# A fused attention and MLP layer on one core: the second MLP weight's block sums made in SBUF instead of DRAM

## The chip, the cores and the metric

The kernel runs on one core of one Trainium2 chip. The metric is the device time of one launch in microseconds (us), lower is better. Times before are the median of three runs; beside them one execution was taken by the hardware profiler, and all rows of the trace come from that one.

## The reference

One layer over 512 frames of width 1024, in float32. `w1` is 1024 x 4096, `w2` is 4096 x 1024.

```python
hn = rmsnorm(h, norm_mix_g[l])
proj = hn @ w_in[l]
fq, fk, fv, ff, gq, gf, gi, gg = jnp.split(proj, split_idx, axis=-1)
...
fox_out = fox_attention(to_heads(fq), to_heads(fk), to_heads(fv), log_f)   # 8 heads of 64, causal, log-forget bias
rec = hgrn2_chunkwise(gq, gf, gi, lbs[l])                                  # gated linear recurrence, 4 heads
...
h = h + jnp.concatenate([fox_out, rec], axis=-1) @ w_out[l]
h = h + memory_cross_attention(rmsnorm(h, norm_x_g[l]), mem_n, w_xq[l], w_xkv[l], w_xo[l])
u = rmsnorm(h, norm_ff_g[l]) @ w1[l]
h = h + jnp.square(jax.nn.relu(u)) @ w2[l]
return rmsnorm(h, final_norm_g)
```

## The kernel before

Every matrix product runs in three passes on TensorE (PE): operands are split into a high part and a low part of a 32-bit format that PE multiplies faster (`float32r`), and high x high, high x low and low x high are added up in PSUM. So every weight that comes from DRAM is loaded raw by a DMA on SP's queue, its high part is made by ScalarE (ACT, line 178) and its low part by VectorE (DVE, line 182). Four buffers hold the high parts (`wh`) and four the low parts (`wl`); a split can start when the product four units earlier has left its buffers.

The stages follow one another on PE, whose order is written out by hand: the projections by `w_in` with the recurrence, the forgetting attention (softmax in 16 steps of two heads, with projections and the memory's keys and values run between as filler), `w_out`, the cross attention, and the MLP. The order on the other engines is made by a scheduler at build time.

The MLP's hidden width of 4096 is cut into eight groups of 512. For groups 2 to 7 the product with `w1` ("u"), and for all groups the product with `w2` ("d"), are computed by a scheme with seven block products instead of eight (`PRODUCTS`, in the order 1, 5, 6, 2, 7, 3, 4). Three of the seven take a plain quarter of the weight block, 00, 10 or 11 (`QUAD`); the other four take sums of quarters: "5" is 00+01, "7" is 01+11, "6" is 5+11, "4" is 6+10 (`SUMS`). On PE the order is: the "u" products of group g+1, then the "d" products of group g. Groups 6 and 7 of "d" are interleaved at the end.

The sums of weights do not depend on the input, and before the change all are made by DMAs from DRAM to DRAM, issued by GpSimd (POOL): `sum_jobs` gives eight DMAs for each group and weight, a copy (line 427) and an accumulation (line 425) for each of the four sums, 512 KB each. `Presum` paces them: `tick` counts PE's matmul time, and `PACE` says from which count on one goes out how often.

```python
RAWS, HB, LOADS = 5, 4, 7
PACE = (25.0, 4.0), (106.0, None), (183.0, 3.0), (306.0, 6.0)
```

In the attention loop, where the pace is off, each of the 16 steps issues one instead. Each sum DMA waits for the PE instruction at which it was counted. POOL also makes the softmax's bias rows (`fox_bias`), small powers, sums of squares, and the output's first scaling (`fa`, line 1599).

In the MLP, `unit` hands out split weights: it prepares four units ahead and loads seven ahead (`LOADS`), raw blocks going to five buffers in turn, two of the pool `wr` and three of the shared pool `s4` (twelve buffers of 512 KB, which also hold the accumulators, hidden parts `hb` and much else). `hidden_sums` combines the squared hidden values on DVE for the seven products, `add_to` adds a product's PSUM bank to the accumulators; banks U, V and Y take several products each (`PLAN`), and a copy of U to V is made by ACT after product "1".

Small pools: `q2` holds four tiles of 256 KB (the queries' parts, later the final gain `gfin`), `t3` two.

Of the kernel before, what the change touches and what calls it, by code (L numbers as in the profile page):

```python
# [9 lines left out]
F32 = mybir.dt.float32  # L10
R = mybir.dt.float32r
# [26 lines left out]
X1, X2, X3, X4 = 1.5, 2.0, 1.5, 2.0  # L38
NEG = -3.0e38
SEVEN = (2, 3, 4, 5, 6, 7)  # L40
RAWS, HB, LOADS = 5, 4, 7
PACE = (25.0, 4.0), (106.0, None), (183.0, 3.0), (306.0, 6.0)


@with_exitstack
def emit(
# [32 lines left out]
    ap_ = ctx.enter_context(tc.tile_pool(name="ap", bufs=4))  # L79
    s4p = ctx.enter_context(tc.tile_pool(name="s4p", bufs=12))  # L80
    k4p = ctx.enter_context(tc.tile_pool(name="k4p", bufs=4))
    q2p = ctx.enter_context(tc.tile_pool(name="q2p", bufs=4))
    t3p = ctx.enter_context(tc.tile_pool(name="t3p", bufs=2))
    t2p = ctx.enter_context(tc.tile_pool(name="t2p", bufs=10))
    s3p = ctx.enter_context(tc.tile_pool(name="s3p", bufs=3))
    smp = ctx.enter_context(tc.tile_pool(name="smp", bufs=16))
# [12 lines left out]
    def k4(shape, name, dt=F32):  # L99
        return k4p.tile([P] + shape, dt, tag="k4", name=name)  # L100

    def q2(name):
        return q2p.tile([P, S], R, tag="q2", name=name)

    def t3(name):
        return t3p.tile([P, S], F32, tag="t3", name=name)

    def t2(name, dt=F32, shape=(S,)):
        return t2p.tile([P] + list(shape), dt, tag="t2", name=name)
# [344 lines left out]
            return us  # L454

    presum = Presum()
    for g in range(DFF // HG):
        presum.jobs.append(sum_jobs("d", g))
        if g + 2 in SEVEN:
            presum.jobs.append(sum_jobs("u", g + 2))  # L460
    park = {}

    ms0 = sm(NT, "ms0")
# [344 lines left out]
    def fox_proj(p):  # L808
        wt = next_panel()

        fq[p] = [q2(f"q{p}{j}") for j in range(2)]
        ps = mm(f"pq{p}")
        yield from gemm_fm(ps, wt, 0, hn_hi, hn_lo)
        t = t3(f"qs{p}")
# [11 lines left out]
        t = t3(f"ks{p}")  # L826
# [25 lines left out]
    def fox_rows(p):  # L852
        for h in (2 * p, 2 * p + 1):
            fF[h] = t2(f"nF{h}")
            ac.dma_start(fF[h], Fd[h, :].partition_broadcast(P))

    mt = []

# [198 lines left out]
    for n in range(len(pairs) + 2):  # L1057
        if n < len(pairs):
            p, tb = pairs[n]
            if tb == 0:  # L1060
                fill.until(f"proj{p}")
                if p == 0:
                    fill.add(proj_tm(new_fv(), WT, AF.Identity, "fv"), "fv256")
                    fill.add(fox_proj(2), "proj2")
                elif p == 1:
                    fill.add(mem_v(0))
                    fill.add(fox_proj(3), "proj3")
                elif p == 2:
                    fill.add(mem_v(1))
                    for i in range(4):  # L1070
                        fill.add(mem_k(i))
        if n >= 3 and n % 2 == 1:
            for step in pairs[n - 3 : n - 1]:
                fox_out(*step)
        if 1 <= n <= len(pairs):
            for j in range(2):
                fox_T((*pairs[n - 1], j))
        if n == 0:
            me_hi.extend(s4([4, M], f"meh{t}", R) for t in range(2))
            me_lo.extend(s4([4, M], f"mel{t}", R) for t in range(2))  # L1080
        elif n <= KC // 2:
            mem_T(2 * n - 2)
        if n < len(pairs):
            fox_scores(*pairs[n])
            if n + 1 < len(pairs):
                fox_biases(n + 1)
            dma = presum.emit()
            if dma is not None:
                tc.keep_in_program_order(dma)
            if tb == 2 and p < 3:  # L1090
                fox_rows(p + 1)
        fill.run(FX[min(n // NT, 1)][n % NT])
# [75 lines left out]
    def x_proj(h):  # L1168
        wt = next_panel()
        xq[h] = []  # L1170
        for i in range(2):
            ps = mm(f"xq{h}{i}")
            yield from gemm_fm(ps, wt, i * P, x1_hi, x1_lo)
            a, b = q2(f"xqh{h}{i}"), q2(f"xql{h}{i}")
# [101 lines left out]

    gfin = [q2p.tile([P, S], F32, tag="q2", name=f"gfin{i}") for i in range(2)]
    for i in range(2):  # L1280
        gp.dma_start(gfin[i], final_norm_g[i * S : (i + 1) * S].partition_broadcast(P))
    HS = S // 2
    units, unit_q = {}, deque()
    sqs, comb, hbs = {}, {}, {}
# [3 lines left out]

    def raw_tile(name):
        raw_n[0] += 1  # L1290
        if raw_n[0] % RAWS in (0, 2):
            return wrp.tile([P, D], F32, tag="wr", name=f"wr{name}", padded_shape=[P, UK * UW])
        return s4([D], f"wr{name}")

    load_q = deque()

    def add_unit(key, shape, src):

        name = "".join(map(str, key))
        box = []  # L1300

        def load():
            raw = raw_tile(name).rearrange("p (k n) -> p k n", k=shape[0])
            nc.sync.dma_start(raw, src())
            box.append(raw)

        def prep():
# [313 lines left out]
    def mlp_up_group(g):  # L1621
# [3 lines left out]
        for j in range(2):  # L1625
# [72 lines left out]
```

## Time and profile before

| | |
|---|---|
| median of 3 timed runs | 766.57 us (764.31 to 767.61) |
| the profiled execution, its own time | 761.13 us |
| its span, first to last instruction | 759.4 us |
| PE busy | 747.1 us (98%) |
| DVE, ACT, POOL busy | 533.4, 429.9, 227.0 us |
| mean granted TensorE clock | 0.999 |
| DMA moved | 162.86 MB, 64.52 of it by POOL's queue |

How to read the rows: a group row has line, engine, operation, output <- input, and after the x the number of instructions; a DMA row has the size of one and the median time from issue to landing; a row of a stretch has its bounds, its length, then for PE, PEld (the weight load), DVE, ACT and POOL the busy time and the number of instructions, then the granted clock, the DMA engines' busy share and GB/s. In the chain and the timeline a row starts with its start and its duration. A row of the waits gives the total, the number and the longest. Tile names have their numbers cut: `wrd` is a raw block of `w2`, `wru` of `w1`, `whd` and `wld` its high and low part, `wsd` and `wsu` sums in DRAM, `hb` a hidden part, `nF` a bias row, `mt` the memory, `bi` and `pt` the softmax and its transpose.

### The profile page before, as it was taken

What the parts mean: (1) busy time and instruction counts of PE and PEld (TensorE: products, weight loads), DVE (VectorE), ACT (ScalarE), POOL (GpSimd) and SP (SyncE); (2) the same over time, 40 slices, a digit from 0 to 9 for tenths busy, and PEclk for the clock granted to TensorE, in tenths of its full rate; (3) what the DMA queues carried; (4) which work ended last, traced back from release to release, by engine and by line L of the source; (5) the groups of instructions that cost most, each with busy time, mean ns of one, the idle gap of its engine ahead of it and who ended that gap; (6) DMA issues with size and microseconds to landing.
All of it is one profiled execution on the core that took longest, in us unless ns stands there. A gap on an engine that the chain in (4) does not pass through costs nothing.

```text
span 759.4 us, 12056 instructions
## 1 busy us (share of the span) xinstructions
PE 747.1 (98%) x4501; PEld 649.1 (85%) x4501; DVE 533.4 (70%) x844; ACT 429.9 (57%) x715; POOL 227.0 (30%) x322
## 2 busy tenths in 40 slices
PE   9999999999998999999999999999999999999996
PEld 6889888898887988888888888898989999998985
DVE  5647873676876755545555558888788787979697
ACT  5655564565664643335443476657575757574873
POOL 7218552353453426841112211111111110000014
PEclk9999999999999999999999999999999999999999
DMA  8676877676788799996679969898988998948342
GB/s 249 195 222 132 209 191 167 183 159 159 194 255 216 232 221 265 236 253 152 151 212 182 242 159 306 178 356 220 289 263 290 226 291 267 274 146 276 113 139 111
DMA packets 99580, 162.86 MB, mean 214 GB/s; under 512 B 6481, under 2 KB 67450, under 8 KB 99074
## 3 DMA queue, kind: packets, MB, share of 16 engines
q0 software_dynamic: 27968, 64.52, 38.9%
q1 hardware_dynamic: 69810, 94.43, 37.4%
q10 hardware_dynamic: 1744, 3.15, 1.3%
q8 instruction: 35, 0.57, 0.3%
q14 instruction: 23, 0.19, 0.1%
HBM read 157.87 MB, written 62.93 MB: 291 GB/s over the span
## 4 chain that ended last, share of the span: by engine, by line
PE 95%; DMA 2%; DVE 1%; ACT 1%; issue 1%; POOL 0%; ACTq 0%; SPq 0%
PE U L1504 4%; PE U L1503 4%; PE U L1505 4%; PE uU L1378 3%; PE uU L1377 3%; PE uU L1376 3%; PE xq L243 2%; PE wo L243 2%; PE xq L244 2%; PE xq L245 2%; PE xw L245 2%; PE xw L244 2%; PE xw L243 2%; PE u L245 2%; PE wo L244 2%; PE u L244 2%
## 5 line engine op out<-in xcount | busy, mean ns | idle before, releaser
L182 DVE TENSOR_TENSOR wld<-wrd,whd 128x1024 fp32r<-128x1024 f32 x56 | 68.5, 1225 | 19.4 <-ACT whd L178 19.4
L178 ACT ACTIVATE whd<-wrd 128x1024 fp32r<-128x1024 f32 x56 | 59.2, 1057 | 26.1 <-PE uV L1377 8.0
L425 POOL DMA_DIRECT2D wsd<-in_w_dram x32 | 34.7, 1084 | 104.0 <-PE uU L1378 22.1
L178 ACT ACTIVATE whu<-wru 128x1024 fp32r<-128x1024 f32 x42 | 44.4, 1057 | 36.5 <-PE uU L1377 16.6
L182 DVE TENSOR_TENSOR wlu<-wru,whu 128x1024 fp32r<-128x1024 f32 x42 | 50.5, 1228 | 12.8 <-ACT whu L178 12.8
L1503 PE MATMUL U<-whd,hb 128*128 128x512 f32 x120 | 46.8, 390 | 0.0
L1504 PE MATMUL U<-wld,hb 128*128 128x512 f32 x120 | 46.8, 390 | 0.0
L1505 PE MATMUL U<-whd,hb 128*128 128x512 f32 x120 | 46.7, 389 | 0.0
L425 POOL DMA_DIRECT2D wsu<-in_w_dram x24 | 28.5, 1186 | 53.9 <-PE xq L245 8.7
L987 POOL TENSOR_SCALAR bi<-nF,Ft 128x128 f32<-128x128 f32 (+3 forms) x32 | 22.5, 707 | 47.2 <-PE pt L1019 26.0
L1599 POOL TENSOR_TENSOR fa<-acc,gfin 128x512 f32<-128x512 f32 x4 | 6.5, 1654 | 86.2 <-DVE acc L1469 83.9
L427 POOL DMA_DIRECT2D wsd<-in_w_dram x16 | 10.9, 680 | 56.8 <-PE gq L245 14.5
L1378 PE MATMUL uU<-x_hi,wlu 128*128 128x256 f32 x96 | 27.2, 283 | 0.0
L1377 PE MATMUL uY<-xs_lo,whu 128*128 128x256 f32 x96 | 27.2, 283 | 0.0
L1378 PE MATMUL uU<-xs_hi,wlu 128*128 128x256 f32 x96 | 27.2, 283 | 0.0
L1376 PE MATMUL uY<-xs_hi,whu 128*128 128x256 f32 x96 | 27.2, 283 | 0.0
L1378 PE MATMUL uY<-xs_hi,wlu 128*128 128x256 f32 x96 | 27.2, 283 | 0.0
L1376 PE MATMUL uU<-xs_hi,whu 128*128 128x256 f32 x96 | 27.2, 283 | 0.0
L1377 PE MATMUL uU<-xs_lo,whu 128*128 128x256 f32 x96 | 27.2, 283 | 0.0
L1377 PE MATMUL uU<-x_lo,whu 128*128 128x256 f32 x96 | 27.2, 283 | 0.0
L1376 PE MATMUL uU<-x_hi,whu 128*128 128x256 f32 x96 | 27.1, 283 | 0.0
L1133 ACT ACTIVATE x_hi<-hT,gv 128x512 fp32r<-128x512 f32 x16 | 11.4, 715 | 27.5 <-DVE hT L1132 27.4
(996 smaller groups left out, 2679.4 us busy)
## 6 DMA issues: line engine op xcount, KB each, us to landing
wsd<-in_w_dram POOLq DMA_DIRECT2D x48, 512.0 KB, 6.5
wsu<-in_w_dram POOLq DMA_DIRECT2D x36, 512.0 KB, 6.7
wrd<-wsd SPq DMA_DIRECT2D x32, 512.0 KB, 5.2
wrd<-in_w_dram SPq DMA_DIRECT2D x24, 512.0 KB, 6.1
wru<-wsu SPq DMA_DIRECT2D x24, 512.0 KB, 4.8
wru<-in_w_dram SPq DMA_DIRECT2D x18, 512.0 KB, 5.9
wsd<-wsd POOLq DMA_DIRECT2D x16, 512.0 KB, 5.5
wsu<-wsu POOLq DMA_DIRECT2D x12, 512.0 KB, 5.1
```

What stands on the lines that cost most here:

```text
L178: ac.activation(hi, raw, AF.Copy)
L182: ve.tensor_tensor(lo, raw, f(hi), ALU.subtract)
L243: te.matmul(ps, wh, hi, start=n_ == 0 and not begun, stop=False)
L244: te.matmul(ps, wh, lo, start=False, stop=False)
L245: at = te.matmul(ps, wl, hi, start=False, stop=k == order[-1])
L425: yield gp.dma_start(dst, block(g, b), accum_op=ALU.add)
L1376: te.matmul(ps[:, i, :], whi[:, k, ws], xh[:, k, :], start=begin, stop=False, skip_group_check=True)
L1377: te.matmul(ps[:, i, :], whi[:, k, ws], xl[:, k, :], start=False, stop=False, skip_group_check=True)
L1378: at = te.matmul(ps[:, i, :], wlo[:, k, ws], xh[:, k, :], start=False, stop=k == UK - 1, skip_group_check=True)
L1503: te.matmul(ps, hi, whi[:, k, :], start=begin, stop=False, skip_group_check=True)
L1504: te.matmul(ps, hi, wlo[:, k, :], start=False, stop=False, skip_group_check=True)
L1505: at = te.matmul(ps, lo, whi[:, k, :], start=False, stop=k == 1, skip_group_check=True)
```

## The change

W2 sums of groups 0 to 6 are no longer made in DRAM. `chain_begin(g)` loads five blocks of `w2` into SBUF (`a1` and `c1` = 00, `a2` = 01, `b2` = 11, `b1` = 10) and accumulates `a2 += 11` and `c1 += 01` from DRAM by POOL's DMAs. The split of product "1" reads `a1`; then `a1 += a2` makes the sum for "6" in place. The split of "2" reads `b1`; then `b1 += a1` makes the sum for "4". "5" reads `c1`, "7" reads `a2`, "3" reads `b2`. A chain begins when the first "u" unit of group g+1 is prepared, and group 0's before the MLP starts.

W1 sums of groups 2 to 7 and the W2 sums of group 7 stay in DRAM. `PACE` starts them at a count of 183, past the attention, every 3 us, and from 306 on every 10 us; the attention loop issues none. At most three raw loads (`RAWS`) wait for their split, in two buffers of `wr` and one of `s4`.

The pools `q2` and `t3` become `q4` (two tiles of 512 KB) and `t4` (one), which also hold `b1` and `b2`. The bias rows `nF` are loaded by POOL's queue and no longer by ACT's, the final gain by one DMA.

```diff
-RAWS, HB, LOADS = 5, 4, 7
-PACE = (25.0, 4.0), (106.0, None), (183.0, 3.0), (306.0, 6.0)
+RAWS, HB = 3, 4
+PACE = (183.0, 3.0), (306.0, 10.0)
...
-    q2p = ctx.enter_context(tc.tile_pool(name="q2p", bufs=4))
-    t3p = ctx.enter_context(tc.tile_pool(name="t3p", bufs=2))
+    q4p = ctx.enter_context(tc.tile_pool(name="q4p", bufs=2))
+    t4p = ctx.enter_context(tc.tile_pool(name="t4p", bufs=1))
...
-    for g in range(DFF // HG):
-        presum.jobs.append(sum_jobs("d", g))
-        if g + 2 in SEVEN:
-            presum.jobs.append(sum_jobs("u", g + 2))
+    for g in SEVEN:
+        presum.jobs.append(sum_jobs("u", g))
+    presum.jobs.append(sum_jobs("d", NG - 1))
...
-            ac.dma_start(fF[h], Fd[h, :].partition_broadcast(P))
+            gp.dma_start(fF[h], Fd[h, :].partition_broadcast(P))
...
-            dma = presum.emit()
-            if dma is not None:
-                tc.keep_in_program_order(dma)
...
-        if raw_n[0] % RAWS in (0, 2):
+        if raw_n[0] % RAWS:
             return wrp.tile([P, D], F32, tag="wr", name=f"wr{name}", padded_shape=[P, UK * UW])
         return s4([D], f"wr{name}")
...
         def prep():
             while not box:
                 load_q.popleft()()
+            if key[0] == "u" and key[1] not in chain:
+                chain_begin(key[1] - 1)
+            waiting[0] -= 1
...
+    chain = {}
+    RAW = {"1": "a1", "2": "b1", "5": "c1", "3": "b2", "6": "a1", "7": "a2", "4": "b1"}
+
+    def chain_begin(g):
+
+        chain[g + 1] = w = {}
+        for name, rc in (("a1", "00"), ("c1", "00"), ("a2", "01"), ("b2", "11"), ("b1", "10")):
+            if name == "b2":
+                t = t4(f"wb2{g}")
+            elif name == "b1":
+                t = q4(f"wb1{g}", F32)
+            else:
+                t = s4([2, S], f"w{name}{g}")
+            w[name] = t
+            nc.sync.dma_start(t, block2(g, rc))
+        gp.dma_start(w["a2"], block2(g, "11"), accum_op=ALU.add)
+        gp.dma_start(w["c1"], block2(g, "01"), accum_op=ALU.add)
+
+    def add_chain(g, name):
+
+        def prep():
+            w = chain[g + 1]
+            unit = new_parts([2, S], f"d{g}{name}")
+            with ahead(PW):
+                split_of(unit[0], unit[1], w[RAW[name]])()
+            if name == "1":
+                gp.dma_start(w["a1"], w["a2"], accum_op=ALU.add)
+            elif name == "2":
+                gp.dma_start(w["b1"], w["a1"], accum_op=ALU.add)
+            units["d", g, name] = unit
+
+        unit_q.append((("d", g, name), prep))
...
     def down_units(gs):
         for name in PRODUCTS:
             for g in gs:
+                if g < NG - 1:
+                    add_chain(g, name)
+                    continue
                 add_unit(("d", g, name), [2, S], lambda g=g, name=name: block2(g, QUAD[name]) if name in QUAD else wsum["d", g, name])
...
-        while load_q and len(order) - len(load_q) < at + LOADS:
+        while load_q and waiting[0] < RAWS:
             load_q.popleft()()
...
+    chain_begin(0)
     ups = mlp_up_group(0)
```

More of the change, by code (lines that the diff above doesn't have):

```diff
@@ L100, in k4, with q4, t4 @@
         return k4p.tile([P] + shape, dt, tag="k4", name=name)
[L102 to L106, printed above, removed]
+    def q4(name, dt=R):
+        return q4p.tile([P, 2, S], dt, tag="q4", name=name)
+    def t4(name):
+        return t4p.tile([P, 2, S], F32, tag="t4", name=name)
     def t2(name, dt=F32, shape=(S,)):
@@ L809, in fox_proj @@
         wt = next_panel()
-        fq[p] = [q2(f"q{p}{j}") for j in range(2)]
+        q, ts = q4(f"q{p}"), t4(f"qk{p}")
+        fq[p] = [q[:, j, :] for j in range(2)]
         ps = mm(f"pq{p}")
         yield from gemm_fm(ps, wt, 0, hn_hi, hn_lo)
-        t = t3(f"qs{p}")
+        t = ts[:, 0, :]
         ve.scalar_tensor_tensor(t, ps, 0.125, rbc, op0=ALU.mult, op1=ALU.mult)
@@ L825, in fox_proj @@
         yield from gemm_fm(ps, wt, P, hn_hi, hn_lo)
-        t = t3(f"ks{p}")
+        t = ts[:, 1, :]
         ve.tensor_tensor(t, ps, rbc, ALU.mult)
@@ L1173, in x_proj @@
             yield from gemm_fm(ps, wt, i * P, x1_hi, x1_lo)
-            a, b = q2(f"xqh{h}{i}"), q2(f"xql{h}{i}")
+            ab = q4(f"xq{h}{i}")
+            a, b = ab[:, 0, :], ab[:, 1, :]
             ac.activation(a, ps, AF.Copy)
@@ L1269, in emit @@
     run_now(rest())
-    gfin = [q2p.tile([P, S], F32, tag="q2", name=f"gfin{i}") for i in range(2)]
-    for i in range(2):
-        gp.dma_start(gfin[i], final_norm_g[i * S : (i + 1) * S].partition_broadcast(P))
+    gfin = q4("gfin", F32)
+    gp.dma_start(gfin.rearrange("p h n -> p (h n)"), final_norm_g.partition_broadcast(P))
+    gfin = [gfin[:, i, :] for i in range(2)]
     HS = S // 2
@@ L1290, in raw_tile @@
         raw_n[0] += 1
-        if raw_n[0] % RAWS in (0, 2):
+        if raw_n[0] % RAWS:
             return wrp.tile([P, D], F32, tag="wr", name=f"wr{name}", padded_shape=[P, UK * UW])
         return s4([D], f"wr{name}")
-    load_q = deque()
+    load_q, waiting = deque(), [0]
     def add_unit(key, shape, src):
@@ L1305, in load @@
             box.append(raw)
+            waiting[0] += 1
         def prep():
```

## The prediction

> **What bounds the kernel now.** I read the page first, then who TensorE (PE) waited for, the table of stretches, the chain that ended last, the DMA issues, and last the rows of one MLP group.
>
> ```profile
> span 759.4 us, 12056 instructions
> PE 747.1 (98%) x4501; PEld 649.1 (85%) x4501; DVE 533.4 (70%) x844; ACT 429.9 (57%) x715; POOL 227.0 (30%) x322
> ```
>
> PE works 747.1 of 759.4 us. The change touches no matmul: in the built program PE's instructions stand in the same order as before. So it can only win back PE's idle time, 12.3 us, or add to it. Where that idle time lies, first by what ended it, then by stretch (in each row the second number is the stretch, the third PE's busy time):
>
> ```profile
> PE pt L1019 <- DVE dn L1010: 3.1, 1, 3.1
> PE pst L906 <- DVE rec L927: 1.5, 1, 1.5
> PE warm L355 <- DVE ones L359: 1.3, 1, 1.3
> ...
> 125.00:150.00 25.00, 23.37 (x146) 20.35 (x145) 13.98 (x32) 13.10 (x41) 8.43 (x14) 1.00 0.54 170
> 225.00:250.00 25.00, 21.95 (x155) 19.20 (x155) 17.36 (x40) 14.10 (x28) 9.08 (x16) 1.00 0.80 214
> 575.00:600.00 25.00, 25.00 (x191) 24.16 (x190) 17.72 (x21) 17.18 (x24) 3.15 (x3) 1.00 0.99 286
> 750.00:760.00 10.00, 3.16 (x26) 2.91 (x24) 4.96 (x12) 2.78 (x5) 1.82 (x4) 0.88 0.56 210
> ```
>
> PE has two holes in mid-kernel, 1.63 us (25 - 23.37) and 3.05 us (25 - 21.95), both before the MLP. The rest is the first and the last microseconds, which the change leaves as they are. In the MLP, of which 575 to 600 is a sample, PE has no hole at all: the list above names no other wait. The granted clock is 1.00 in all these stretches but the last. The chain shows what made the two holes (start, duration):
>
> ```profile
> 118.07 0.63 POOL wsu L425
> 118.70 8.46 DMA mt<-in_mem_dram
> 134.64 1.13 PE pst L906 x8
> 231.12 8.23 DMA wr19a<-in_w_xkv_dram
> 239.37 1.07 ACT wh19a L178
> 243.50 1.22 PE pt L1019 x8
> ```
>
> Both are late transfers. The load of `mt` is queued on POOL behind a block sum (L425), travels 8.46 us, and holds up ScalarE (ACT) on the way to `pst`. The load of `wr19a` travels 8.23 us; ACT stands at its split, and the softmax behind it on ACT comes late for `pt`.
>
> **Part by part: sums taken out of the way of the attention.**
>
> ```profile
> wsd<-in_w_dram POOLq DMA_DIRECT2D x48, 512.0 KB, 6.5
> wsu<-in_w_dram POOLq DMA_DIRECT2D x36, 512.0 KB, 6.7
> wrd<-wsd SPq DMA_DIRECT2D x32, 512.0 KB, 5.2
> wrd<-in_w_dram SPq DMA_DIRECT2D x24, 512.0 KB, 6.1
> ...
> wsd<-wsd POOLq DMA_DIRECT2D x16, 512.0 KB, 5.5
> wsu<-wsu POOLq DMA_DIRECT2D x12, 512.0 KB, 5.1
> nF<-Fd ACTq DMA_DIRECT2D x8, 256.0 KB, 4.7
> ```
>
> Before: 48+36+16+12 = 112 sum DMAs. After: 8 for each of the six W1 groups and 8 for W2 group 7, 56, and the first of them stands on POOL behind the last softmax bias. So all sums that run beside the projections and the attention go, and the two late loads have the engines of the DMA more to themselves. Neither hole should survive a load that comes some 3 us sooner: 1.63 + 3.05 = 4.7 us gained. What is late next: in the first place nothing, since ACT was waiting for `mt` alone; in the second the bias rows `nF`, which move from the ACT queue to POOL. They land in 4.7 us by the row, and their issue on POOL costs time in which POOL makes no bias; but POOL is busy 9.08 of 25 us there, so I cost that at nothing (if this cover is gone, some 1 us of the 3.05 stays). One new W2 load (`wb20`) also goes ahead of `wr19a` in SP's queue; its transfer takes the place of sums that are gone. The smaller gain, one hole closed and not the other, is 1.6 us; below nothing there is no mechanism here that the rows show.
>
> From 183 us of counted matmul time on, sums go out every 3 us, the same pace as before, only W1's; PE had no hole in that stretch, and I cost it at nothing. Joining pools (`q2`, `t3`) keeps the bytes and the users in pairs: nothing.
>
> **Part by part: W2 sums made in SBUF.** Per group g of 0 to 6, 8 sum DMAs in DRAM and 7 loads become 5 loads on SP and 4 accumulating DMAs on POOL: 15 transfers become 9, so the MLP's DMA queues get lighter. What is new is a chain within the group. The accumulation `a1 += a2` may start only when the split of product "1" has read `a1`, and the split of "6" must wait for it; `b1 += a1` sits likewise between the splits of "2" and "4". ACT and VectorE (DVE) take their work in order, so a late "6" split delays all that is queued behind it. How long may such a DMA take? Rows of a typical group (its product "1" starts on PE at 597.08):
>
> ```profile
> 589.61 1.23 DVE L182 TENSOR_TENSOR wld<-wrd,whd 128x1024 fp32r<-128x1024 f32 x1 [1.65 <-ACT whd L178]
> 594.29 1.05 ACT L178 ACTIVATE whd<-wrd 128x1024 fp32r<-128x1024 f32 x1
> 599.16 0.62 ACT L1346 ACTIVATE sq<-sq 128x512 f32<-128x512 f32 x1
> 599.81 0.69 DVE L1437 TENSOR_TENSOR s<-sq,sq 128x512 f32<-128x512 f32 x1 [0.34 <-ACT sq L1346]
> 604.81 1.35 DVE L1471 SCALAR_TENSOR_TENSOR acc<-U,acc 128x512 f32<-128x512 f32 x2
> 607.99 0.39 PE L1503 MATMUL U<-whd,hb 128*128 128x512 f32 x1
> 609.60 1.23 DVE L182 TENSOR_TENSOR wld<-wrd,whd 128x1024 fp32r<-128x1024 f32 x1
> 613.42 0.39 PE L1503 MATMUL U<-whd,hb 128*128 128x512 f32 x1
> ```
>
> The split of "1" has read its block at 589.61 + 1.23 = 590.84. The split of "6" starts at 594.29 today; call its start S. From it to the end of the square at 599.16 + 0.62 lie 5.49 us of ACT work, and DVE then works through the hidden sums (from 599.81) to the first subtraction from bank U, which ends half-way through the pair at 604.81, at 605.49: 5.68 us. PE's product "7" writes bank U at 607.99 and must find it read: S + 5.49 + 0.03 + 5.68 <= 607.99, S <= 596.8. The same DVE run on to the low half for "4" (609.60 + 1.23) is 11.02 us, needed 0.23 us after 613.42: S <= 597.1. So from POOL's issue to landing there are 596.8 - 590.84 = 5.9 us free; every us more is a us of PE per group. Of the seven chains five (groups 1 to 5) have this shape; group 0's splits come a whole long panel ahead, and group 6's products are interleaved with group 7's and twice as far apart.
>
> No row shows an accumulation in SBUF. The nearest are these: accumulations in DRAM (L425, whole run, then MLP alone), copies on the same queue (L427), and stores out of SBUF on it (L491); minimum, median and maximum time to landing.
>
> ```profile
> L425 POOL DMA_DIRECT2D wsd<-in_w_dram x32: 1026/1074/1229, 59.9 to 652.2; - x32
> DMA to landing us min/median/max: 6.1/7.6/11.2
> ```
>
> ```profile
> L425 POOL DMA_DIRECT2D wsd<-in_w_dram x11: 1026/1058/1080, 488.1 to 652.2; - x11
> DMA to landing us min/median/max: 6.1/8.1/11.2
> ```
>
> ```profile
> L427 POOL DMA_DIRECT2D wsd<-in_w_dram x16: 607/686/735, 41.0 to 573.3; - x16
> DMA to landing us min/median/max: 3.8/5.2/7.8
> ```
>
> ```profile
> L491 POOL DMA_DIRECT2D xTd<-xT x4: 531/550/804, 14.2 to 29.3; - x4
> DMA to landing us min/median/max: 2.9/3.3/4.5
> ```
>
> The bounds are 2.9 us (the fastest plain transfer of this size out of SBUF) and 11.2 us. My value: a transfer out of SBUF, 3.3, plus what accumulating adds to a copy, 7.6 - 5.2 = 2.4: an estimate of 5.7 us. I stay near it and not near 8.1, because at the time of `a1 += a2` the W2 loads of the group are long done and half the sums are gone. 5.7 lies just inside 5.9; single landings scatter by about 1 us (2.9 to 4.5), so I charge 0.1 us for each of the five groups, 0.5 us. At 2.9 us it costs nothing (a gain is excluded, PE has no hole there); at 8.1 it costs 5 x 2.2 = 11.0 us.
>
> The Trainium skill (DMA: Bandwidth & Descriptors, section "Anatomy of one DMA — SWDGE (gpsimd) path") gives every DMA issued by GpSimd about 2.0 us plus its bytes over 436 GB/s. By it 512 KB would take an estimated 3.2 us and the chain would cost nothing at all, so the sum would be 4.7 us of gain. The L491 row agrees with it, the L425 rows (7.6 us for the same bytes) do not, and what an accumulation within SBUF takes no row here shows; I keep the estimate from the rows.
>
> What waits behind a waiting instruction: on POOL, the next group's two accumulations from DRAM and the remaining W1 and group 7 sums, needed tens of us later; on SP, the next group's loads of `a1` wait until `b1 += a1` has landed, and behind them stand W1 loads. Only three raw buffers are left for these, where there were five; but the W2 loads that shared them are gone, and I cost it at nothing. If each group lost a us there, it would be 5 us, which the range holds.
>
> **Sum.** -4.7 + 0.5 = -4.2 us. The profiled execution took 761.13 us (span 759.4); -4.2 makes it 756.9. The median of the timed runs is 766.57, 5.4 above the profiled one, and the profile does not show why; I take the same 4.2 off it: **762.4 us**, 0.55% faster.
>
> **The rivals.** About 0.5% (3.8 us) is what a measurement of this kernel can tell from no change.
> *A: sums in SBUF land no sooner than sums in DRAM.* For it: the accumulation itself adds 2.4 us whatever the place, and the MLP rows have a median of 8.1. Against it: source and target are both on the core, and the queues are lighter. Price: 5 x (8.1 - 5.9) = 11.0; 766.57 - 4.7 + 11.0 = 772.9 us. It turns slower than before at a landing of 5.9 + 4.7/5 = 6.8 us, and by more than 0.5% at 5.9 + 8.5/5 = 7.6 us.
> *B: gain and loss cancel.* One hole stays, because the bias rows now come through POOL's queue or the panel loads are slow by themselves (the plain loads `wrd<-in_w_dram` also take 6.1 us), so that only 1.6 us are won: 765.0 us; or both close and the accumulations take 6 to 7.6 us. Against it: the two loads that made the holes took 8.46 and 8.23 us, well above 6.1.
>
> **How the numbers follow.** The forecast gets 0.45, B 0.23, A 0.32; the same three numbers are the chances of faster by over 0.5%, within it, and slower by over it, since the forecast and A lie beyond it. Low end: the timed runs were 5.4 us above the profiled one, and if most of that is the same two waits grown longer it goes too: 766.57 - 4.7 - 4 = 758. High end: A with a landing of 8.9 us, some of the slower rows: 5 x 3.0 = 15.0, 766.57 - 4.7 + 15.0 = 777. The forecast's own range is 758 to 764.
>
> **What would show it.** Right: PE's list of waits loses `pst` and `pt`, `mt` lands in well under 8 us, PE is busy 25.00 of 25 us in every MLP stretch, and the accumulations `wa<-wa` and `wb<-wa` land in under 5.9 us. Wrong: holes of PE in the MLP at "6", "7" or "4", ended by DVE or ACT, with ACT's `whd` waiting for `wa<-wa`; or the holes near 133 and 241 us still there.

## The result and the profile after

The change makes the kernel slower: 807.89 us (804.51 to 808.48) against 764.67 us (763.36 to 767.61) for the kernel before in the same session, ratio 1.0546, 95% interval 1.0515 to 1.0576. The forecast was 762.4 us, 0.5% faster. The profiled execution took 807.47 us, its span is 46.4 us longer than before. Three executions of the runs below (2643.37, 1245.18 and 791.02 us) were disturbed, and medians and ratios leave them out.

The head of the page, PE's list of waits, and six stretches of the kernel after:

```profile
span 805.8 us, 11988 instructions
PE 761.4 (95%) x4501; PEld 659.2 (82%) x4501; DVE 534.2 (66%) x844; ACT 428.2 (53%) x715; POOL 215.6 (27%) x301
```

```profile
PE uU L1414 <- ACT uV L1420: 28.3, 5, 8.5
PE uU L1414 <- ACT uY L1425: 3.8, 2, 2.5
...
PE U L1541 <- DVE acc L1509: 1.2, 2, 0.6
...
PE pt L1019 <- DVE bi L1011: 0.7, 1, 0.7
```

```profile
125.00:150.00 25.00, 25.00 (x160) 22.31 (x159) 15.71 (x34) 14.87 (x49) 7.40 (x13) 1.00 0.31 93
150.00:175.00 25.00, 24.31 (x169) 22.38 (x168) 16.91 (x45) 15.15 (x38) 9.71 (x22) 1.00 0.20 61
225.00:250.00 25.00, 24.95 (x188) 22.19 (x188) 20.01 (x49) 15.84 (x33) 9.32 (x18) 1.00 0.58 181
500.00:525.00 25.00, 19.42 (x141) 19.02 (x140) 9.94 (x10) 11.03 (x15) 1.65 (x2) 0.86 0.85 221
550.00:575.00 25.00, 16.50 (x127) 16.30 (x126) 10.82 (x11) 11.33 (x16) 2.49 (x3) 0.86 0.87 219
600.00:625.00 25.00, 21.18 (x142) 20.45 (x141) 10.32 (x11) 12.58 (x17) 1.96 (x2) 0.86 0.76 217
```

The attention did what was forecast. Both holes are gone, the one of `pst` and the one of `pt` near 241 us (24.95 of 25 us), and `mt`, which travelled 8.46 us, now lands in 3.6. The 0.7 us that the list still has at `pt` is a new hole near 164 us, in a stretch (150 to 175) where PE had none before. PE's instructions stand in the same order in both kernels, so the same matmul can be compared: the one that started at 246 us before starts 4.1 us sooner.

From there to the MLP's sevenfold products 2.0 us of this are lost again, in small waits. These products, from 496 us on, then lose 47.7 us (from 2.1 us ahead to 45.6 behind). The MLP now has a hole in every group of "u", always ahead of a product that reuses bank U: in five groups "6" (in the first of them "7" as well, 1.2 us), in one "7". PE waits there for ACT's copy of U to V (or Y). And the granted clock, 1.00 before, is 0.86 in these stretches. The copy itself takes 0.58 us; what ACT does ahead of it is seen in its rows at the longest hole (the product "1" of this group starts at 545.67), with SP's rows below:

```profile
543.26 1.05 ACT L178 ACTIVATE whu<-wru 128x1024 fp32r<-128x1024 f32 x1
545.87 0.63 ACT L1490 ACTIVATE hb<-n 128x512 fp32r<-128x512 f32 x1 [1.57 <-PE U L1543]
557.55 2.00 ACT L178 ACTIVATE whu<-wru 128x1024 fp32r<-128x1024 f32 x2 [11.04 <-DMA wru<-in_w_dram]
559.46 0.58 ACT L1420 ACTIVATE uV<-uU 128x512 f32<-128x512 f32 x1
```

```profile
536.34 0.38 SPq L1334 DMA_DIRECT2D wa<-in_w_dram  x1
536.82 0.48 SPq L1334 DMA_DIRECT2D wc<-in_w_dram  x1
537.40 0.41 SPq L1334 DMA_DIRECT2D wa<-in_w_dram  x1
539.18 0.37 SPq L1334 DMA_DIRECT2D wb<-in_w_dram  x1
540.00 0.34 SPq L1302 DMA_DIRECT2D wru<-wsu  x1
542.11 0.37 SPq L1334 DMA_DIRECT2D wb<-in_w_dram  x1
545.04 6.27 SPq L1302 DMA_DIRECT2D wru<-in_w_dram  x3
```

ACT's queue has the splits of "2" and "7" ahead of the copy. The split of "2" stands idle for 11.04 us until its raw W1 block lands. SP issued that load at 545.04, when "1" of the same group was about to start on PE, because only then a raw buffer came free, and after the five loads of the next chain (L1334) had gone out; it landed at 557.5. So "6", whose own weights were ready, waits for a copy that waits for a block that "6" does not use.

The time to landing (minimum, median, maximum) of W1 raw blocks, first before, then after. The profile shows it for 11 of the 42 blocks in each, and for no more than that in the runs below:

```profile
DMA to landing us min/median/max: 3.2/5.3/8.2
```

```profile
DMA to landing us min/median/max: 3.3/7.4/12.4
```

It is not that more is moved: the whole kernel moves 140.84 MB, where it was 162.86. From 480 to 705 us, before and after:

```profile
480.00:705.00 225.00, 225.00 (x1430) 205.30 (x1429) 185.75 (x228) 145.08 (x193) 23.21 (x27) 1.00 0.85 255
```

```profile
480.00:705.00 225.00, 193.75 (x1145) 174.31 (x1144) 151.43 (x187) 114.85 (x155) 29.14 (x29) 0.93 0.76 204
```

The DMA engines are less busy on average (0.76 against 0.85), but the transfers come in bursts: in the six microseconds in which the late block of the group above is issued they are full (share 1.03, first row). Full engines alone are not the trouble, though. The kernel before has stretches as full (second row) without a hole, with five raw buffers:

```profile
545.00:551.00 6.00, 6.00 (x49) 5.88 (x48) 5.88 (x9) 0.63 (x1) 2.27 (x2) 1.00 1.03 261
546.00:552.00 6.00, 6.00 (x53) 6.00 (x52) 2.45 (x2) 3.72 (x5) 1.19 (x1) 1.00 1.08 334
```

The accumulations within SBUF, which the prediction worried about, mostly landed in time (`a1 += a2`, then `b1 += a1`):

```profile
L1346 POOL DMA_DIRECT2D wa<-wa x7: 877/917/1036, 469.3 to 754.1; - x7
DMA to landing us min/median/max: 4.5/4.8/7.5
```

```profile
L1348 POOL DMA_DIRECT2D wb<-wa x7: 852/865/882, 480.0 to 772.2; - x7
DMA to landing us min/median/max: 4.5/4.5/6.1
```

Two of the seven `a1 += a2` took longer than the 5.9 us allowed (7.45 and 7.00). In these two groups ACT's split of "6" waits for them, and PE then stands 0.6 us ahead of a "d" product for DVE's `acc`, as the prediction had said; that is the 1.2 us in the list above.

### The profile page after: what moved, and what is told of

It reads as the page before. It is cut to its first block, busy times and chain, and to the rows that moved or that the text cites. A ratio compares the mean times of both kernels' runs of the same rounds, so it can differ in the third digit from the quotient of the medians.

```text
span 805.8 us, 11988 instructions
## 1 busy us (share of the span) xinstructions
PE 761.4 (95%) x4501; PEld 659.2 (82%) x4501; DVE 534.2 (66%) x844; ACT 428.2 (53%) x715; POOL 215.6 (27%) x301
## 2 busy tenths in 40 slices
DMA packets 94572, 140.84 MB, mean 175 GB/s; under 512 B 5793, under 2 KB 66762, under 8 KB 94290
## 5 line engine op out<-in xcount | busy, mean ns | idle before, releaser
L1414 PE MATMUL uU<-xs_hi,whu 128*128 128x256 f32 x96 | 32.9, 343 | 32.1 <-ACT uV L1420 28.3
L1414 PEld LDWEIGHTS uU<-xs_hi,whu 128*128 128x128 f32 x96 | 23.1, 241 | 33.5 <-ACT uV L1420 29.3
L182 DVE TENSOR_TENSOR wld<-wa,whd 128x1024 fp32r<-128x1024 f32 x21 | 25.7, 1222 | 16.2 <-ACT whd L178 16.1
L178 ACT ACTIVATE whd<-wa 128x1024 fp32r<-128x1024 f32 x21 | 22.1, 1051 | 18.4 <-DMA wa<-wa 8.9
L1415 PE MATMUL uU<-xs_lo,whu 128*128 128x256 f32 x96 | 31.7, 330 | 0.0
L1416 PE MATMUL uU<-xs_hi,wlu 128*128 128x256 f32 x96 | 31.5, 328 | 0.0
L1346 POOL DMA_DIRECT2D wa<-wa x7 | 6.4, 920 | 88.7 <-DVE wld L182 88.7
L182 DVE TENSOR_TENSOR wld<-wb,whd 128x1024 fp32r<-128x1024 f32 x21 | 26.8, 1274 | 4.5 <-ACT whd L178 4.5
L1541 PEld LDWEIGHTS U<-whd,hb 128*128 128x128 f32 x120 | 22.5, 188 | 8.5 <-issue 2.1
```

The source lines that it names most:

```text
L178: ac.activation(hi, raw, AF.Copy)
L182: ve.tensor_tensor(lo, raw, f(hi), ALU.subtract)
L1346: gp.dma_start(w["a1"], w["a2"], accum_op=ALU.add)
L1414: te.matmul(ps[:, i, :], whi[:, k, ws], xh[:, k, :], start=begin, stop=False, skip_group_check=True)
L1415: te.matmul(ps[:, i, :], whi[:, k, ws], xl[:, k, :], start=False, stop=False, skip_group_check=True)
L1416: at = te.matmul(ps[:, i, :], wlo[:, k, ws], xh[:, k, :], start=False, stop=k == UK - 1, skip_group_check=True)
```

## The experiments

Theories for the 47.7 us lost in the MLP: T1, three raw buffers are too few; T2, W1 loads stand behind the chain's loads in SP's queue; T3, the chain's seven transfers come as a burst and fill the DMA engines just when W1 blocks are needed. The W2 sums' landing in SBUF is rival A of the prediction. The ratios are to the kernel before, measured beside each run.

**All sums late, but in DRAM.**

```diff
-PACE = (25.0, 4.0), (106.0, None), (183.0, 3.0), (306.0, 6.0)
+PACE = (183.0, 2.0), (306.0, 5.0)
...
-            dma = presum.emit()
-            if dma is not None:
-                tc.keep_in_program_order(dma)
```

> The kernel before with all its DRAM sums (W1 and W2, 112 transfers) issued past the attention (from 183 us of counted matmul time, one every 2 us, from 306 us one every 5 us) and nothing else of the change: no sums in SBUF, five raw buffers. If the gain came from taking sums out of the attention alone, the holes of 1.63 us (pst) and 3.05 us (pt) go and the MLP keeps its five raw buffers: 760 us, 4 to 5 us below before. Rival: the gain needs the lighter DMA queues of the SBUF sums; then the denser sums between 183 and 306 us make holes of their own, and the time is 765 us or more.

776.92 us, ratio 1.0164 (1.0128 to 1.0200). The rival holds for this pace: both attention holes are gone or small (225 to 250 us is 25.00 of 25), but from 300 to 350 us PE is busy for 41.76 of 50, because POOL's sum of squares comes late among the sums issued every 2 us:

```profile
PE pm L1149 <- POOL ssq L1139: 7.0, 1, 7.0
PE pt L1019 <- DVE bi L1011: 0.7, 1, 0.7
```

The second row is the new hole of the changed kernel: PE is busy 24.31 of 25 us from 150 to 175 here too. The bias rows still come by ACT's queue in this run, so their move to POOL's is not what made it.

Sums taken out of the attention have to go somewhere; here the new place cost more than the old one.

**Five raw buffers** (two more in the pool `wr`; the room comes from `t2` and `sm`).

```diff
-RAWS, HB = 3, 4
+RAWS, HB = 5, 4
-    wrp = ctx.enter_context(tc.tile_pool(name="wrp", bufs=2))
+    wrp = ctx.enter_context(tc.tile_pool(name="wrp", bufs=4))
...
```

> The changed kernel with five raw buffers instead of three (the room is taken from two small pools, so the attention may lose some us). Theory T1, too few raw buffers: a W1 block is loaded when the buffer of the block three products earlier is split, 8.6 us ahead of its use, and lands in 7 to 12 us; with five buffers the load starts 5.8 us sooner, the five holes before product 6 (28.3 us) and the slow matmuls behind them (14 us) go: 760 to 768 us. Theory T3, the DMA engines are full at the start of each group (five loads and two accumulations of the chain beside the W1 loads): the loads are late all the same, and over half of the 46 us stay: above 785 us.

787.56 us, ratio 1.0314 (1.0277 to 1.0350). Between the two. The wait for the copy to V is gone, a part has moved on to the copy to Y, behind the next late split:

```profile
PE uU L1414 <- ACT uY L1425: 13.2, 4, 6.4
PE pv L1035 <- ACT pts L1023: 7.1, 7, 2.0
```

The second row is the price of the smaller pools in the attention (PE 92.15 of 100 us from 175 to 275). Compared matmul by matmul, the MLP alone loses 19.0 us here instead of 47.7. Two buffers more give back 29 us, though W1 blocks take no less time to land (median 9.8 us); they are issued sooner.

**Chain loads on POOL's queue.**

```diff
-            nc.sync.dma_start(t, block2(g, rc))
+            gp.dma_start(t, block2(g, rc))
```

> The changed kernel with the five loads of each chain issued from GpSimd's queue instead of SP's, so that no W1 load stands behind them; three raw buffers as in the change. Theory T2, the W1 loads of products 7 and 2 are late because they stand in SP's queue behind the chain's five loads: the holes go, 760 to 770 us. Theory T1 (a buffer comes free too late) and T3 (DMA engines full): the load of product 2 still waits for its buffer and still takes about 12 us; holes before product 6 stay, 795 to 815 us.

808.47 us, ratio 1.0585 (1.0542 to 1.0629): nothing gained. Compared matmul by matmul the MLP loses 44.0 us instead of 47.7; these 3.7 us are lost again ahead of it, where from 400 to 475 us PE is busy for 71.96 of 75. So T2 is at most a small part: it matters that the transfers are under way at this time, and much less in whose queue they stood.

**ACT's copy ahead of the splits.** The splits of "2" and "7" are prepared one product later and kept behind the copy in ACT's order.

```diff
-        while unit_q and len(order) - len(unit_q) < at + 4:
+        while unit_q and len(order) - len(unit_q) < at + (3 if key[0] == "u" and key[2] == "1" else 4):
...
+                if what == "hl pin":
+                    tc.keep_in_program_order(ins)
```

> The changed kernel with ScalarE's copy of bank U (product 1) put ahead of the splits of products 2 and 7 in ScalarE's queue. If the late raw load reaches PE only through this copy, PE goes on with product 6 (2.9 us) and then stands before product 2 for what is left: each of the five holes becomes 2.9 us shorter and moves from product 6 to product 2 or 7, and product 6 no longer runs at half clock; 785 to 797 us. If the holes had another cause than the late split (the copy itself, or PSUM), they go altogether: below 770 us.

796.71 us, ratio 1.0439 (1.0397 to 1.0481). As expected, at the upper end: the waits are still 25.1 us (32.1 in the change), but now stand further on.

```profile
PE uU L1416 <- ACT uY L1427: 15.6, 5, 5.3
PE uV L1416 <- ACT whu L178: 6.8, 4, 3.7
PE uV L1418 <- DVE wlu L184: 2.7, 4, 0.8
```

The last two rows are "2" waiting for its own split. So the copy only handed the lateness on; that cost 9 us of the 47.7 (the MLP loses 38.7 here, matmul by matmul).

**No chain loads from group 1 on** (constants instead).

```diff
-            nc.sync.dma_start(t, block2(g, rc))
+            if g > 0:
+                gp.memset(t, 0.01)
+            else:
+                nc.sync.dma_start(t, block2(g, rc))
+        if g > 0:
+            return
```

> The changed kernel with the five loads and the two accumulations from DRAM of groups 1 to 6 left out: GpSimd fills the five tiles with a constant instead (so W2 of these groups is not the real one), and the accumulations within SBUF stay. Three raw buffers as in the change, 42 transfers fewer. Theory T1, three raw buffers are too few in themselves (a block is loaded 8.6 us ahead of its use, less some 2.3 us for the two splits, and lands in 7 us or more even without the chain): holes of 1 us or more stay in the MLP, 775 to 800 us. Theory T3, the loads are late only because the chain's seven transfers fill the DMA engines at the start of each group: W1 blocks land in under 6 us, the holes go, 757 to 766 us.

769.16 us, ratio 1.0046 (1.0017 to 1.0074). W1 blocks land in 4.3 us (median), and the longest hole is 1.7 us, still with three buffers:

```profile
PE uU L1419 <- ACT uY L1430: 2.2, 2, 1.1
PE uU L1419 <- ACT uV L1425: 1.7, 1, 1.7
...
DMA to landing us min/median/max: 3.2/4.3/5.6
```

Compared matmul by matmul the MLP loses 8.8 us (from 3.6 ahead to 5.2 behind) instead of 47.7: 39 us of the loss need the chain's transfers. That is what T3 says, but the run takes away the bytes together with the burst (118.81 MB are moved in all, not 140.84), so it cannot tell these two apart. The rest, small holes, is what three buffers leave even without them, somewhat more than T3 alone had forecast.

**No accumulations within SBUF** (both left out).

```diff
-            if name == "1":
-                gp.dma_start(w["a1"], w["a2"], accum_op=ALU.add)
-            elif name == "2":
-                gp.dma_start(w["b1"], w["a1"], accum_op=ALU.add)
```

> The changed kernel with the two accumulations within SBUF of each chain left out (so products 6, 7 and 4 of W2 use blocks without the last addend); all loads stay. This prices rival A of the prediction. By the trace they landed in 4.8 and 4.5 us, within the 5.9 us that the chain allows: 802 to 809 us, nothing gained beyond scatter. If the accumulations were the cost, or held up SP's queue through the buffers that they keep: 795 us or less.

794.02 us, ratio 1.0354 (1.0321 to 1.0386): 14 us gained, where I had expected none. The waits are of the same kind, only shorter, and still ahead of "6" of "u":

```profile
PE uU L1410 <- ACT uV L1416: 22.9, 5, 6.8
```

So the accumulations cost something, though not by landing late ahead of a "d" product. My theory for it was SP's queue, which waits for `b1 += a1` before it can load the next `a1`. A spare block buffer and each accumulation alone were to show it.

**A spare block buffer** (room again from `t2` and `sm`).

```diff
-    s4p = ctx.enter_context(tc.tile_pool(name="s4p", bufs=12))
+    s4p = ctx.enter_context(tc.tile_pool(name="s4p", bufs=13))
```

> The changed kernel with one block buffer more (13 instead of 12; the room is taken from two small pools), so that the first load of the next group's chain need not wait until the accumulation into b1 has read a1. Leaving out the accumulations within SBUF gained 14 us. If that was because SP's queue stands at this wait and issues the burst of chain loads some 3 to 6 us later, into the first W1 loads of the next group: 790 to 798 us here, with the sums still made. If the accumulations cost by their own traffic, or by W2 blocks that come late: 803 us or more.

803.14 us, ratio 1.0514 (1.0469 to 1.0559). This does not tell the two apart: the first load no longer waited for it, but the next tile, `c1`, got the buffer that `a1` had left, and SP stood there from 535.8 to 540.7 us.

**Only `b1 += a1` left out, and only `a1 += a2` left out.**

```diff
-            elif name == "2":
-                gp.dma_start(w["b1"], w["a1"], accum_op=ALU.add)
```

```diff
-            if name == "1":
-                gp.dma_start(w["a1"], w["a2"], accum_op=ALU.add)
-            elif name == "2":
+            if name == "2":
```

> The changed kernel with only the accumulation of a1 into b1 left out (so product 4 of W2 uses a block without the other addends); the one of a2 into a1 stays. In SP's queue the next chain's first load, into a1's buffer, then no longer waits until this accumulation has landed. If the 14 us that both accumulations cost are this wait, which pushes the chain's loads into the next group's first W1 loads: 790 to 799 us. If the cost is another: 803 us or more.

> The changed kernel with only the accumulation of a2 into a1 left out (so products 6 and 4 of W2 use blocks without an addend); the one of a1 into b1 stays, and SP's queue still waits for it. If the wait in SP's queue is the cost, nothing is gained: 802 to 809 us. If the accumulations cost by their landing ahead of product 6: 798 us or less.

803.71 us (ratio 1.0506, 1.0486 to 1.0526) and 799.30 us (1.0438, 1.0392 to 1.0483). Both against my theory: the first gained 4 us where 9 to 18 were forecast, the second 8 to 9 where none was. In the first, SP's wait moved to the second load of the chain once more (same group as above; "1" of "u" starts about 1 us earlier):

```profile
530.91 0.38 SPq L1334 DMA_DIRECT2D wa<-in_w_dram  x1
535.53 0.38 SPq L1334 DMA_DIRECT2D wc<-in_w_dram  x1
536.00 0.42 SPq L1334 DMA_DIRECT2D wa<-in_w_dram  x1
```

With both left out, `c1`'s load goes at 532.13, 11.0 us ahead of "1" of the next group; in the change it goes at 536.82, 8.9 us ahead of it. The load of "2" then goes 2.8 us ahead of "1" instead of 0.6, and takes no less time to land (12.8 us, 12.4 in the change). That fits SP's queue as a part of the cause, but it is one group, and how the 14 us divide into that wait and the accumulations' own traffic stays open.

**Four raw buffers and both copies first; then the chain's transfers spread as well.** The first has `RAWS` 4 (room again from `t2` and `sm`) and the copies after "1" and "6" ahead of the splits of the blocks that follow. The second in addition takes one chain transfer with each product's block of the next group:

```diff
-            if key[0] == "u" and key[1] not in chain:
-                chain_begin(key[1] - 1)
+            if key[0] == "u":
+                if key[1] not in chain:
+                    steps[key[1]] = chain_begin(key[1] - 1)
+                next(steps[key[1]], None)
...
```

> The changed kernel with four raw buffers and with ScalarE's copies of bank U (after products 1 and 6) put ahead of the splits of the next blocks. By T1 and the copies' place in the queue each takes a part of the holes away (five buffers alone gave 787.6 with some 8 us lost in the attention, the copy alone 796.7): 770 to 782 us. If the rest is the burst of the chain's transfers (T3), it cannot reach the kernel before: above 768 us.

> As the run with four raw buffers and ScalarE's copies first (778.3 us), with the chain's seven transfers no longer emitted together but one with each product's block of the next group, so that W1 loads stand between them in SP's queue. If the burst is what is left (T3): 765 to 775 us. If the chain's own needs become late (its accumulations from DRAM start after the loads have landed, and land 9 to 11 us later): W2 blocks hold up the down products, 780 us or more.

778.30 us (ratio 1.0157, 1.0134 to 1.0180) and 774.77 us (1.0120, 1.0096 to 1.0144). Both in their range. Spreading gains some 3 us more (the two intervals just overlap); compared matmul by matmul the MLP loses 16.6 us instead of 22.0, and W1 blocks land in 7.5 us instead of 8.6 (medians). The transfers are the same in both, so this part, some 5 us, is the burst's. What then waits in the spread version is the "d" products, whose largest wait is this:

```profile
PE U L1550 <- ACT V L1560: 5.5, 4, 2.5
```

So sums in SBUF were not brought to the time of the kernel before.

**Three raw buffers in the kernel before.**

```diff
-RAWS, HB, LOADS = 5, 4, 7
+RAWS, HB, LOADS = 3, 4, 7
...
-        if raw_n[0] % RAWS in (0, 2):
+        if raw_n[0] % RAWS:
```

> The kernel before (all sums in DRAM) with three raw buffers instead of five and nothing else; the planner puts some loads in another order. Its loads are spread over the group and land in 4.8 to 6 us, and the lead of three products is 8.6 us less 2.3 us of splits, 6.3 us. If three buffers hurt only where loads land late (T3): 764 to 772 us. If three buffers are too few anyway (T1): holes before many products, 785 us or more.

782.74 us, ratio 1.0233 (1.0179 to 1.0287), some 14 to 22 us more. It lies between the two forecasts, nearer to T1 than I had expected. Three buffers hurt in the old pattern of loads as well, though the planner's other order of loads is in this figure too.

**Pauses put in on purpose** (kernel before).

```diff
+PAUSE = {2: 1, 3: 2, 4: 3, 5: 4, 6: 6}
...
+            if name == "6" and g < 7:
+                for r in range(PAUSE[g]):
+                    hold = gp.memset(qa, 0.0)
...
+                        tc.add_manual_dep(mmul.ins, hold.ins.name, sync, reason="pause")
```

> The kernel before with a pause of TensorE put in on purpose in five MLP groups: ahead of product 6 of groups 2 to 6 it waits for 1, 2, 3, 4 and 6 fills of a tile by GpSimd, which start when product 5 is done. Nothing else is changed and no load is late, so what comes behind the pause is the clock's alone. If a pause costs clock only from some length on (in the changed kernel holes of 2.5 us were followed by none, holes of 3.8 us and more by 3 to 6 us of matmuls at half clock), the short pauses are followed by full clock and the long ones by 3 to 6 us at half clock, whatever their length: the time grows by the pauses and some 2 to 3 us for each long one. If a pause costs only itself: PE's busy time stays at 747 us.

787.74 us in a single execution; PE's busy time is 756.3 us. The stretches of 3 to 4 us right behind the five pauses, which were 1.1, 2.1, 3.1, 4.1 and 6.1 us long:

```profile
509.00:513.00 4.00, 3.48 (x29) 3.48 (x30) 2.71 (x3) 2.36 (x4) 0.98 (x2) 1.00 0.98 363
551.00:555.00 4.00, 3.93 (x32) 3.93 (x33) 0.22 (x1) 0.87 (x1) 0.02 (x1) 1.00 1.05 346
594.00:597.00 3.00, 3.00 (x18) 3.00 (x17) 0.00 (x0) 0.00 (x0) 0.00 (x0) 0.56 0.88 320
639.00:642.00 3.00, 3.00 (x15) 3.00 (x15) 0.00 (x0) 0.00 (x0) 0.00 (x0) 0.50 0.72 275
686.00:690.00 4.00, 4.00 (x20) 4.00 (x21) 0.00 (x0) 0.00 (x0) 0.00 (x0) 0.51 0.00 0
```

Behind the two short pauses the clock is 1.00, behind the three long ones about 0.5. PE loses 0.2 to 0.3 us beyond the short pauses and 1.7, 1.8 and 2.1 us beyond the long ones, where 2 to 3 us were expected. The Trainium skill (TensorE: Matmul & The Clock Gate, section "Part 1: The HAM clock gate (the "warmup" mystery)") says that the clock is halved after a window of some 3.4 us without work and comes back after a like time of work, the windows running on their own. The trace agrees in kind, with 2.1 us unpunished, 4.1 us punished, and 3.2 to 4.2 us of matmuls at half clock each time; but the pause of 3.1 us, shorter than that window, was punished as well.

Near this length it can go either way. The hole at `pt`, 3.05 us long in the kernel before, was followed by full clock there (first row); in this run, 3.25 us long, by half clock for some 6 us (second row), which cost some 2.6 us:

```profile
246.00:248.00 2.00, 2.00 (x19) 2.00 (x19) 1.52 (x9) 1.26 (x5) 1.36 (x4) 1.00 0.47 154
246.00:248.00 2.00, 2.00 (x11) 2.00 (x11) 1.50 (x9) 0.88 (x4) 1.83 (x5) 0.50 0.51 130
```

**No sum in the attention loop, sums otherwise in DRAM** (five raw buffers, W1 and W2 sums as before).

```diff
-PACE = (25.0, 4.0), (106.0, None), (183.0, 3.0), (306.0, 6.0)
+PACE = (25.0, 4.0), (106.0, None), (183.0, 3.0), (306.0, 5.5)
...
-            dma = presum.emit()
-            if dma is not None:
-                tc.keep_in_program_order(dma)
```

> The kernel before, with DRAM sums for W1 and W2 and five raw buffers, but without the one sum that it issued in each step of the attention loop; the sums beside the projections stay, those of the MLP go out every 5.5 us of counted matmul time instead of every 6. If the two holes before the MLP come from the sums of the attention loop alone and a slower pace than in the run with all sums late spares the rows behind the attention: 758 to 761 us, faster than before by 4 to 5 us. Rival: the sums that are moved make holes wherever they go: 764 us or more.

760.45 us (three executions), ratio 0.9928 (0.9902 to 0.9954): 0.7% faster than the kernel before, and faster than the change. The hole at `pt` is gone (25.00 of 25 us from 225 to 250), the one at `pst` stays, and `mt` still travels 8.00 us:

```profile
PE pst L906 <- DVE rec L927: 1.4, 1, 1.4
```

**The same, with sums kept clear of `mt`.**

```diff
-PACE = (25.0, 4.0), (106.0, None), (183.0, 3.0), (306.0, 5.5)
+PACE = (20.0, 2.5), (55.0, None), (183.0, 2.7), (306.0, 5.2)
```

> As the run without sums in the attention loop, but the sums beside the projections go out every 2.5 us of counted time and stop at 55 us, well ahead of the load of mt; from 183 us every 2.7 us, from 306 us every 5.2 us. If the hole before pst (1.4 us there) comes from sums ahead of mt and beside it, it goes too: 757 to 760 us. If the denser pace behind the attention or in the MLP makes holes of its own: 762 us or more.

763.58 us, ratio 0.9983 (0.9961 to 1.0005): no gain over the kernel before is shown. The hole at `pst` is gone as forecast, but the denser sums early on made a larger one among the projections, where the load of `wr5b` took 8.98 us:

```profile
PE dg L704 <- DVE z L671: 3.7, 1, 3.7
```

## Why the prediction was wrong, step by step

**The sums out of the attention: right.** 4.7 us were forecast; the matmuls behind the attention start 4.1 us sooner. Both holes closed, and the difference is the new hole of 0.7 us near 164 us. It is near the 1 us named for the case that the bias rows' cover is gone, but that is chance: it stands at another place, and is there with the bias rows on ACT's queue too. The stretch behind, costed at nothing, lost 2.0 us again, in waits for DVE's `x_lo` among others. The version that only empties the attention loop shows that taking sums out of there is worth having alone.

**The accumulations within SBUF: estimate near, rival A right in kind and small.** Estimated 5.7 us, measured medians 4.8 and 4.5, below the 5.9 allowed. Where one took 7 us or more, PE did wait at the forecast place: 1.2 us in all, where 0.5 was charged and A charged 11.0. None of its holes over 0.6 us stands ahead of a "d" product. That the kernel got slower, as A says, is luck for A: it came by another mechanism. The 3.2 us that follow from the Trainium skill's rule (DMA: Bandwidth & Descriptors, section "Anatomy of one DMA — SWDGE (gpsimd) path") were too low by 1.3 us at least: no accumulation landed in under 4.5 us. The accumulations still cost 14 us, through the loads of the next group; that was in no term of the sum, and how it comes about is shown only in part.

**The step that failed** is this sentence: "Only three raw buffers are left for these, where there were five; but the W2 loads that shared them are gone, and I cost it at nothing. If each group lost a us there, it would be 5 us". Measured: 47.7 us over the six groups with such products, 8.0 each. The reason given counted the users of the buffers and not the lead. With three buffers a block is loaded three products of 2.9 us ahead, and the two splits take 2.3 us of these 8.6; so it has 6.3 us to land. Blocks landed in up to 8.2 us before, and then had two products more. The step beside it, "15 transfers become 9, so the MLP's DMA queues get lighter", held on average and failed where it counted: seven transfers of the next chain go out together at the end of a group, and the W1 blocks of that time took up to 12.4 us. The runs show that most of it takes both: without the chain's transfers 9 us of the 48 remain, with two buffers more 19; and three buffers alone, in the kernel before, cost some 14 to 22. That last part could be read ahead from the profile before, by its slowest landing of 8.2 us against 6.3. Of the chain's part some 5 us are shown to be its burst, with four buffers and the copies first; how the rest divides between burst and bytes stays open.

The prediction had also named SP's queue ("behind them stand W1 loads") as the place of trouble; taking the chain's loads out of that queue gave back 3.7 of the 47.7 us, and nothing in all.

**The missing term** is the clock. The sum reckoned every late transfer at its own length. Five of the seven holes (3.8 to 8.5 us) are followed by 3.1 to 6.3 us of matmuls at half clock, 24 us together, of which 10.9 are lost (each matmul against the same one before). That is most of the 14.3 us by which PE's busy time grew. It may also be what the prediction could not see in the 5.4 us between the profiled execution and the timed runs: of the 40 executions of the kernel before that were taken beside the experiments, the ten shortest (up to 764.11 us) had a mean granted clock of 0.995 to 0.999, and eight of the ten longest (from 766.62 us) 0.994 or less. That is not shown: of these no profile says where the clock was lost.

**What was to show it.** Of the signs for "right", the two holes went and `mt` landed sooner; three of the 14 accumulations took more than 5.9 us (7.5, 7.0 and 6.1), and the MLP stretches of 25.00 did not come. The signs listed for "wrong" named `whd` waiting for `wa<-wa`; that came too (8.9 us of ACT in four waits), but the large holes of PE were `whu` waiting for `wru<-in_w_dram`.

## What to carry to other kernels

Before buffers are taken from a load, work out its lead (buffers times the length of a product, less the work on the block) and hold it against the slowest landing in the trace, not against the median and not against the bytes moved; fewer transfers in a burst can land later than more of them spread out. Look in each in-order queue for what stands behind the instruction that will wait: here a copy of 0.58 us carried a late block to a product that did not need it. And when two parts of a change have nothing to do with each other, price them and try them apart; here the smaller one alone was the gain.

## What the runs showed of the hardware

A pause of TensorE is not paid by its length alone: up to 2.1 us it cost hardly more than itself (0.2 to 0.3 us), and from 3.1 us on another 1.7 to 2.1 us, because 3 to 4 us of matmuls at half clock followed. In the changed kernel holes of 3.8 to 8.5 us cost 1.6 to 3.0 us beyond themselves, and not the more the longer they were. One hole of 3.05 us, in the kernel before, was followed by full clock. An accumulating DMA from SBUF to SBUF of 512 KB landed in 4.5 to 7.5 us; one that adds a block from DRAM into SBUF took longer (the first row is `c1 += 01`, the second `a2 += 11`; the last number is the median time to landing), more than the 8.1 us of the DRAM accumulations that it replaced. These stood in the chain's burst, and no run has them alone.

```profile
wc<-in_w_dram POOLq DMA_DIRECT2D x7, 512.0 KB, 9.0
wa<-in_w_dram POOLq DMA_DIRECT2D x7, 512.0 KB, 11.3
```
